# MLP of a GLA layer on one core: four rounds of 2048 hidden channels in two stages, or eight rounds of 1024 with the two projections interleaved

## The chip, the core and the metric

One NeuronCore of a Trainium2 chip. TensorE (PE) multiplies a stationary 128x128 block with moving columns and adds up in PSUM, eight banks of 128x512 float32. VectorE (DVE) and ScalarE (ACT) read PSUM and SBUF, GpSimd (POOL) does a few small things, and SyncE (SP) issues most DMAs. The metric is the device time of one execution in microseconds; lower is better.

## The reference

A gated linear attention layer and a squared-ReLU MLP over 256 tokens of width 2048, in float32. The change is in the MLP alone:

```python
def _sq_relu_mlp(h, w_up, w_down):
    a = jax.nn.relu(h @ w_up)
    return (a * a) @ w_down
...
        h = h + _sq_relu_mlp(_rmsnorm(h, mlp_norm[i]), mlp_w_up[i], mlp_w_down[i])
    return _rmsnorm(h, final_norm)
```

`w_up` is 2048 x 8192, `w_down` 8192 x 2048.

## The kernel before, in words

**Three matmuls per product.** Each float32 operand is split into a rounded part `hi` (a cast on ScalarE, L110 or L135) and a rest `lo` (a subtraction on VectorE, L111 or L136). A product is hi·hi + hi·lo + lo·hi, three matmuls of 256 columns. `halves` (L142) cuts wider products into such pieces. A weight tile (two row blocks of 512 columns, or one of 1024: 512 KB) is loaded by SP into half of one of three `raw` pairs and split into one of five slots `hi`/`lo` (`weights`, `parts`, `slots`).

**The up projection** (`turned`, L169) computes 512 hidden channels, transposed, in two banks: eight steps of two row blocks, 24 matmuls a step. `gap` stores the second half of a step's weight tile 16 elements further on; `even` lists the steps that do so. Then `up` (L622) forms the stationary blocks: for each 256 channels a ReLU and scale out of PSUM on VectorE (L628), a square on ScalarE (L632), three subtractions that make the sums (L636 to L638), and a split (L640, L641) into `act`.

**The down projection** works on units of 256 hidden channels by 512 columns, a 2x2 by 2x2 block product with 256 tokens. Plain, it takes eight block products. By sums (Strassen's method in Winograd's form) it takes seven, of sums of blocks: four sums on the stationary side (S1 to S4), four on the weight side (`u`, L680 to L685), which are split like any weights. The results lie in banks by which output block they belong to (`b32`, `b74`, `b16`, `b5`), and what can't be added at once is kept in `sums` and joined at the end (L715 to L723).

**Order.** Four rounds `r` of 2048 hidden channels. In each, `up` runs for all four groups of 512 channels; then `down` runs for the left half of the output columns and then the right one, eight hidden pairs each. In a half the first 512 columns go by sums and the second 512 plain (`blocks`, L668), 45 matmuls a pair. In round 3 the right half goes plain, as a last stage (`last_step`) that holds back its last six row blocks so that the columns come to an end one after the other, are normed and stored. Side work (transposes of h, the norm's scale, the joining) waits in a queue `side`; `pump` takes one item behind the latest split, `flush` all that are left. A framework turns the program into a fixed order per engine, by program order and its own estimate of when things are ready, and adds the semaphores.

Of the kernel before, what the change touches and what calls it, by code (L numbers as in the profile page):

```python
# [32 lines left out]
P = 128  # L33
# [28 lines left out]
ROUNDS = HID // D  # L62
# [5 lines left out]
def tile_gla_mlp(ctx, tc, x, xt, cols, w_vg, w_in, w_gate, w_out, w_up, w_down, final_norm, out):  # L68
# [7 lines left out]
    st = ctx.enter_context(tc.tile_pool(name="st", bufs=4))  # L76
# [92 lines left out]
    def turned(row, w, c0, even=(0,), acc=None):  # L169

        acc = acc or acc_banks(GT // P // 2)
        for kp in range(KT // 2):
            wh, wl = weights(w[2 * kp * P : 2 * (kp + 1) * P, c0 : c0 + GT].rearrange("(i p) c -> p i c", p=P), 2 * GT, gap=kp in even)
            for i in range(2):
                kt = 2 * kp + i
                ah, al = row(kt)
                for j in range(GT // P):
                    s = slice(j * P, (j + 1) * P)
                    o = acc[j // 2][:, j % 2 * T : (j % 2 + 1) * T]
                    for n, (u, m) in enumerate(((wh, ah), (wh, al), (wl, ah))):  # L180

                        nc.tensor.matmul(  # L182
                            o, u[:, i, s], m, start=kt == 0 and n == 0 and j % 2 == 0,
                            stop=kt == KT - 1 and n == 2, skip_group_check=True,
                        )
                if kt < KT - 1:
                    pump()
        return acc
# [44 lines left out]
    xe = mid.tile([P, 2, P], F32R, tag="xe", name="xe")  # L233
# [109 lines left out]
    gt = mid.tile([GR, T], F32R, tag="gt", name="gt")  # L343
# [240 lines left out]
    sums = [big.tile([P, 4, T], F32, tag="E" + i, name="sums", bufs=1) for i in "hl"]  # L584
    turned_h = lambda kt: [a[:, kt, :].rearrange("p (t s) -> p t s", t=NT) for a in (hth, htl)]
# [30 lines left out]
    A11, A12, A21, A22, S3, S1, S2, S4 = range(8)  # L616
    KP = KT // 2
    work = mid.tile([P, 3 * G + T], F32, tag="qt", name="work")
    r2row = work[:, 3 * G :]
    work = work[:, : 3 * G].rearrange("p (b c) -> p b c", b=3)  # L620

    def up(r, q, act):  # L622
        acc = turned(lambda kt: (hth[:, kt], htl[:, kt]), w_up, r * D + q * GT, even=() if q > 1 or r > 0 and q else (5,) if r == q == 0 else (0,))
        flush()
        f = work[:, 2].rearrange("p (f s) -> p f s", f=8)
        for b in range(2):
            s = tmp.tile([P, 2, T], F32, tag="t512", name="su", bufs=3)
            nc.vector.scalar_tensor_tensor(  # L628
                s, acc[b].rearrange("p (i t) -> p i t", i=2), 0.0, r2row.unsqueeze(1).to_broadcast([P, 2, T]),
                op0=ALU.max, op1=ALU.mult,  # L630
            )
            nc.scalar.activation(  # L632
                f[:, :4].rearrange("p (t i) s -> p i t s", t=2), s.rearrange("p i (t s) -> p i t s", t=2), AF.Square
            )
            sub = lambda o, x, y: nc.vector.tensor_tensor(o, x, y, op=ALU.subtract)
            sub(f[:, S3 : S1 + 1], f[:, A21 : A21 + 1].to_broadcast([P, 2, P]), f[:, A11 : A22 + 1 : 3])  # L636
            sub(f[:, S2], f[:, A11], f[:, S1])
            sub(f[:, S4], f[:, A12], f[:, S2])  # L638
            oh, ol = (act[q][:, b, i].rearrange("p f s -> p (f s)") for i in range(2))
            nc.scalar.copy(oh, work[:, 2])  # L640
            nc.vector.tensor_tensor(ol, work[:, 2], oh.bitcast(F32), op=ALU.subtract)  # L641

    def stationary(act, kp, f):
        return [act[kp // 2][:, kp % 2, i, f] for i in range(2)]
# [4 lines left out]
    def down(r, half, act):  # L649

        c0 = half * G
        plain = [aux_bank(), aux_bank()] if half == 0 else acc_banks(2)
        b32, b74 = acc_banks(2) if half == 0 else [aux_bank(), aux_bank()]
        b16, b5 = acc_banks(2)
        left, right = slice(0, T), slice(T, 2 * T)
        used = set()

        def product(bank, o, a, w, m, last):

            for i, (x, y) in enumerate(((0, 0), (0, 1), (1, 0))):  # L660
                halves(bank[:, o], a[x], w[y][:, m], bank.name not in used, last and i == 2)
                used.add(bank.name)

        for kp in range(KP):
            last = kp == KP - 1
            at = lambda f: stationary(act, kp, f)
            w = rows(w_down, c0, G, r * D)
            blocks = lambda i, wi: [  # L668
                product(plain[t], slice(0, 512), at((A11, A21)[t] + i), wi, slice(512, G), last and i == 1) for t in range(NT)
            ]  # L670
            assert not raw_half
            pair = wpool.tile([P, 2 * WMAX], F32, tag="raw", name="raw", bufs=3)
            raw0, raw1 = pair[:, :WMAX], pair[:, WMAX:]
            w0 = weights(w(2 * kp), G, skip=T, raw=raw0)
            product(b16, left, at(A11), w0, right, last)
            blocks(0, w0)
            pump()
            w1 = weights(w(2 * kp + 1), G, raw=raw1)
            u = work[:, kp % 2].rearrange("p (f s) -> p f s", f=4)
            add = lambda o, x, y: nc.vector.tensor_tensor(o, x, y, op=ALU.add)  # L680

            both = pair[:, T : T + 2 * (WMAX - T)].rearrange("p (k c) -> p k c", k=2)[:, :, :T]
            add(u[:, :2], raw0[:, left].unsqueeze(1).to_broadcast([P, 2, T]), both)
            add(u[:, 2], u[:, 0], raw1[:, left])
            add(u[:, 3], u[:, 2], raw1[:, right])  # L685
            wu = parts(work[:, kp % 2], G, slots())
            product(b32, right, at(A12), w1, right, last)
            product(b32, left, at(S4), w1, left, last)
            blocks(1, w1)
            product(b5, left, at(S1), wu, slice(0, T), last)  # L690
            product(b74, left, at(S3), wu, slice(T, 2 * T), last)
            product(b16, right, at(S2), wu, slice(2 * T, 3 * T), last)
            product(b74, right, at(A22), wu, slice(3 * T, G), last)
            if not last:
                pump()
        flush()
        for t in range(NT):
            take(plain[t], t, c0 + 512, 512)

        e = sums[half]  # L700
        take(b32, 0, c0, 512)
        if r == 0:
            nc.scalar.copy(e[:, 1:3].rearrange("p b c -> p (b c)"), b16)
            nc.scalar.copy(e[:, 0], b5[:, left])
            nc.scalar.copy(e[:, 3], b74[:, left])
        else:
            both = e[:, 1:3].rearrange("p b c -> p (b c)")
            nc.vector.tensor_tensor(both, b16, both, op=ALU.add)
            nc.vector.tensor_tensor(e[:, 0], b5[:, left], e[:, 0], op=ALU.add)
            nc.vector.tensor_tensor(e[:, 3], b74[:, left], e[:, 3], op=ALU.add)  # L710
        take(b74[:, right], 1, c0 + T, T)
        if r < ROUNDS - 1 - half:
            return

        tt = lambda o, x, y, op: nc.vector.tensor_tensor(e[:, o], e[:, x], e[:, y], op=op)  # L715
        tt(2, 1, 2, ALU.subtract)
        tt(0, 0, 2, ALU.subtract)
        for t in range(NT):
            if t == 1:
                tt(1, 2, 3, ALU.subtract)  # L720
# [109 lines left out]
```

## Time and profile before

| | |
|---|---|
| median of 3 runs | 1071.22 us (1070.77 to 1071.77) |
| the profiled execution | 1071.97 us, span 1070.0 us |
| TensorE busy | 1060.5 us, 9262 matmuls |
| VectorE busy | 780.3 us |
| ScalarE busy | 579.5 us |
| HBM read | 206.92 MB, 195 GB/s over the span |

TensorE's busy time is made of modelled ends of pipelined matmuls, so 99% does not yet say that matmuls follow each other closely: their starts do. The attention takes the first 382 us. The MLP's stages, in us from the start of the span: up of round 0 until about 472, then down and up alternate (down until 553, up until 640, down until 722, up until 809, down until 891, up until 978), then the last left half until about 1017 and the last stage. In rows of the timeline and the chain the first number is the start, the second the length.

### The profile page before, as it was taken

Reading aid. Unit: us, or ns where it says so; the run is one execution under the profiler, and the core shown is the slowest. Engines: PE = TensorE matmul, PEld = TensorE weight load, DVE = VectorE, ACT = ScalarE, POOL = GpSimd, SP = SyncE. Lnnn points to the kernel's source line nnn. Section 1 sums busy time; section 2 is a strip of 40 time slices with the busy share of each in tenths; the row PEclk is TensorE's granted clock in tenths of the full one; section 3 lists DMA queues with packets and bytes.
Section 4 is the critical chain, followed back from the end, with each engine's and each line's share of the span. In section 5 each row is a group of like instructions: output and inputs, shape, how many; then the busy total and the mean of one; then the engine's idle time right before and its main releaser. Section 6 shows DMA issues by size and latency. Waiting matters only on the chain.

```text
span 1070.0 us, 21834 instructions
## 1 busy us (share of the span) xinstructions
PE 1060.5 (99%) x9262; PEld 1059.9 (99%) x9262; DVE 780.3 (73%) x1039; ACT 579.5 (54%) x699; POOL 12.7 (1%) x39
## 2 busy tenths in 40 slices
PE   9999999999999999999999999999999999999997
PEld 9999999999999999999999999999999999999997
DVE  7578645556555566789976689986779997678984
ACT  7585444546444454555654556554546554555652
POOL 0000000000000000000000000000000000000000
PEclk9999999999999999999999999999999999999998
DMA  9847654556545555546565555566654566555662
GB/s 337 305 158 219 189 191 151 165 154 193 196 163 194 192 166 196 197 160 225 208 222 191 191 185 198 197 214 220 197 197 160 198 234 213 191 193 177 227 221 79
DMA packets 79569, 210.43 MB, mean 197 GB/s; under 512 B 6720, under 2 KB 7616, under 8 KB 79344
## 3 DMA queue, kind: packets, MB, share of 16 engines
q1 hardware_dynamic: 78512, 206.99, 58.5%
q10 hardware_dynamic: 960, 2.05, 0.5%
q8 instruction: 72, 1.18, 0.4%
q14 instruction: 25, 0.20, 0.1%
HBM read 206.92 MB, written 2.10 MB: 195 GB/s over the span
## 4 chain that ended last, share of the span: by engine, by line
PE 98%; issue 1%; DMA 0%; DVE 0%; ACT 0%; SPq 0%; POOLq 0%; POOL 0%; DVEq 0%; ACTq 0%
PE acc L147 44%; PE acc L182 39%; PE aux L147 12%; PE aux L182 2%; PE aux L533 1%; PE aux L462 1%; DMA raw<-in_w_vg 0%; PE acc L363 0%; DVE hf L789 0%; ACT sqf L742 0%; DVE h L647 0%; ACT hi L110 0%; POOLq L826 0%; POOL rf L297 0%; PE aux L608 0%
## 5 line engine op out<-in xcount | busy, mean ns | idle before, releaser
L111 DVE TENSOR_TENSOR lo<-raw,hi 128x1024 fp32r<-128x1024 f32 (+2 forms) x225 | 256.7, 1143 | 117.1 <-ACT hi L110 115.2
L110 ACT CAST hi<-raw 128x1024 fp32r<-128x1024 f32 (+2 forms) x225 | 222.1, 987 | 208.4 <-PE acc L147 122.4
L182 PE MATMUL acc<-hh,hi 128*128 128x256 f32 x1024 | 283.2, 277 | 0.0
L182 PE MATMUL acc<-hh,lo 128*128 128x256 f32 x1024 | 283.1, 276 | 0.0
L182 PE MATMUL acc<-hl,hi 128*128 128x256 f32 x1024 | 283.0, 276 | 0.0
L136 DVE TENSOR_TENSOR lo<-raw,hi 128x1024 fp32r<-128x1024 f32 x160 | 195.6, 1223 | 115.9 <-ACT hi L135 115.2
L135 ACT CAST hi<-raw 128x1024 fp32r<-128x1024 f32 x160 | 168.1, 1051 | 186.6 <-PE acc L182 142.2
L147 PE MATMUL acc<-hi,act 128*128 128x256 f32 x1200 | 218.1, 276 | 0.0
L182 PEld LDWEIGHTS acc<-hh,hi 128*128 128x128 f32 x1024 | 192.3, 188 | 0.0
L182 PEld LDWEIGHTS acc<-hh,lo 128*128 128x128 f32 x1024 | 192.3, 188 | 0.0
L182 PEld LDWEIGHTS acc<-hl,hi 128*128 128x128 f32 x1024 | 192.3, 188 | 0.0
L147 PEld LDWEIGHTS acc<-hi,act 128*128 128x128 f32 x1200 | 180.9, 188 | 0.0
L147 PE MATMUL acc<-lo,act 128*128 128x256 f32 x600 | 143.2, 276 | 0.0
L147 PE MATMUL aux<-hi,act 128*128 128x256 f32 x704 | 133.7, 276 | 0.0
L147 PE MATMUL acc<-hi,xA 128*128 128x256 f32 x736 | 106.9, 282 | 0.6 <-ACT hi L110 0.6
L147 PEld LDWEIGHTS aux<-hi,act 128*128 128x128 f32 x704 | 106.6, 188 | 0.0
L147 PEld LDWEIGHTS acc<-lo,act 128*128 128x128 f32 x600 | 102.4, 188 | 0.0
L147 PEld LDWEIGHTS acc<-hi,xA 128*128 128x128 f32 x736 | 95.2, 190 | 1.1 <-ACT hi L110 0.9
L110 ACT CAST hi<-work 128x1024 fp32r<-128x1024 f32 x56 | 59.1, 1056 | 37.5 <-PE aux L147 13.9
L147 PE MATMUL aux<-lo,act 128*128 128x256 f32 x352 | 76.3, 276 | 0.0
L111 DVE TENSOR_TENSOR lo<-work,hi 128x1024 fp32r<-128x1024 f32 x56 | 68.3, 1220 | 9.4 <-ACT hi L110 7.5
L147 PE MATMUL acc<-lo,xA 128*128 128x256 f32 x368 | 60.1, 281 | 0.0
(162 smaller groups left out, 1275.9 us busy)
## 6 DMA issues: line engine op xcount, KB each, us to landing
raw<-in_w_up SPq DMA_DIRECT2D x128, 512.0 KB, 4.5
raw<-in_w_down SPq DMA_DIRECT2D x128, 512.0 KB, 4.4
raw<-in_w_in SPq DMA_DIRECT2D x80, 512.0 KB, 4.6
raw<-in_w_out SPq DMA_DIRECT2D x32, 512.0 KB, 4.1
raw<-in_w_vg SPq DMA_DIRECT2D x13, 520.0 KB, 8.7
h<-in_x SPq DMA_DIRECT2D x4, 512.0 KB, 7.2
zz<-in_xt SPq DMA_DIRECT2D x3, 384.0 KB, 7.9
fb<-in_final_norm ACTq DMA_DIRECT2D x1, 1024.0 KB, 7.0
```

Of the source, the lines that this page charges most:

```text
L110: last_hi[0] = nc.scalar.copy(hi[:, s], raw[:, s])
L111: last_lo[0] = nc.vector.tensor_tensor(lo[:, s], raw[:, s], hi[:, s].bitcast(F32), op=ALU.subtract)
L135: last_hi[0] = nc.scalar.copy(to[0], dst)
L136: last_lo[0] = nc.vector.tensor_tensor(to[1], dst, to[0].bitcast(F32), op=ALU.subtract)
L147: nc.tensor.matmul(o[:, m], x, w[:, m], start=first and c == 0, stop=last, skip_group_check=True)
L182: nc.tensor.matmul(o, u[:, i, s], m, start=kt == 0 and n == 0 and j % 2 == 0, stop=kt == KT - 1 and n == 2, skip_group_check=True,)
L462: nc.tensor.matmul(o, kab[:, k[0], c0 + c, k[1] : k[1] + P], q(qt[:, c0 + c]), start=c == 0, stop=c == 1)
L533: nc.tensor.transpose(b[:, i * T + t * P : i * T + (t + 1) * P], src[:, t, kt * P : (kt + 1) * P], ident)
```

## The change

A round now has 1024 hidden channels, two groups of 512 of the up projection and four hidden pairs; there are eight rounds. `turned` becomes a generator that yields after each of its eight steps (`turned_steps`), and `up` runs through all rounds with it. `down` is a generator too: it walks through passes (round, column group of 512), in alternating direction, and yields after each unit of four per pass. A loop first takes 18 up steps and then one up step behind every unit, until the up steps are used up. The up groups after the first collect in the two `aux` banks instead of two of the six `acc` banks; a pass uses four `acc` banks, which stay in use where a round starts with the column group that the last one ended with. Which units go by sums is given by `by_sums`: the first three of four hidden pairs, two in column group 1, and three of the eight units in round 7. Each column group has its own `sums` tile; its four banks are emptied with four operations of 512 columns. Columns 1024 and up of round 7 are the last stage, eight row blocks, six of them held. The blocks of `act` are in another order so that pairs which go plain need only half of it. `xe` and `gt` share one tile, and the ring `st` has three buffers instead of four.

```diff
+MR = 2 * GT
+ROUNDS = HID // MR
...
-    st = ctx.enter_context(tc.tile_pool(name="st", bufs=4))
+    st = ctx.enter_context(tc.tile_pool(name="st", bufs=3))
...
+    def turned_steps(row, w, c0, even, acc, flip=0):
         for kp in range(KT // 2):
             wh, wl = weights(w[2 * kp * P : 2 * (kp + 1) * P, c0 : c0 + GT].rearrange("(i p) c -> p i c", p=P), 2 * GT, gap=kp in even)
...
+                    k = j % 2 ^ flip
+                    o = acc[j // 2][:, k * T : (k + 1) * T]
...
                 if kt < KT - 1:
                     pump()
+            yield
...
+    sums += [mid.tile([P, 4, T], F32, tag=i, name="sums") for i in ("db", "ee")]
...
+    def order_of(m):
+
+        return range(GROUPS)[:: 1 if m % 2 else -1]
+
+    def by_sums(m, g, kp):
+
+        if m == ROUNDS - 1:
+            return (g, kp) in ((0, 0), (0, 2), (1, 0))
+        return kp < (2 if g == 1 else 3)
+
+    def up():
+        for m in range(ROUNDS):
+            for q in range(MR // GT):
+                first = m == q == 0
+                acc = acc_banks(2) if first else [aux_bank(), aux_bank()]
+                even = (5,) if first else (0,) if m == 0 else (3,) if q == 0 else ()
+                yield from turned_steps(lambda kt: (hth[:, kt], htl[:, kt]), w_up, m * MR + q * GT, even, acc, 1)
+                if m == 0:
+                    flush()
...
+                for b in range(2):
+                    forms(m, 2 * q + b, acc[b], act[:, b])
+
+    def forms(m, kp, bank, act):
+        ways = {by_sums(m, g, kp) for g in range(GROUPS)}
...
+        if True in ways:
...
+            sub(f[:, S3 : S1 + 1], f[:, A21:].to_broadcast([P, 2, P]), f[:, A11 : A22 + 1])
+            sub(f[:, S2], f[:, A11], f[:, S1])
+            sub(f[:, S4], f[:, A12], f[:, S2])
...
+        some = slice(0 if True in ways else A12, 8 if False in ways else A21)
...
+    def down(passes):
+
+        for n, (m, g) in enumerate(passes):
+            if not n or passes[n - 1][1] != g:
+                b32, bx4, b16, b57 = acc_banks(4)
+            ends = n + 1 == len(passes) or passes[n + 1][1] != g
+            for kp in range(KP):
...
+                src = w_down[c0 : c0 + 2 * P, g * GT : (g + 1) * GT].rearrange("(i p) c -> p i c", p=P)
+                last_load[0] = nc.sync.dma_start(out=raw.rearrange("p (i c) -> p i c", i=2), in_=src)
+                if not by_sums(m, g, kp):
+                    w = parts(raw, 2 * GT, slots())
+                    for i in range(2):
+                        for bank, f in ((b32, (A11, A12)), (bx4, (A21, A22))):
+                            product(bank, slice(0, GT), at(f[i]), w, slice(i * GT, (i + 1) * GT))
+                    yield
+                    continue
+                w = parts(raw, 2 * GT, slots(), [(T, 2 * GT)])
...
+                add(u[:, :2], raw[:, :1].to_broadcast([P, 2, T]), raw[:, 1:3])
+                add(u[:, 2], u[:, 0], raw[:, 2])
+                add(u[:, 3], u[:, 2], raw[:, 3])
+                wu = parts(wk, G, slots())
...
+                product(b16, left, at(A11), w, block(1))
+                product(b32, right, at(A12), w, block(3))
+                product(b32, left, at(S4), w, block(2))
+                product(b57, left, at(S1), wu, block(0))
+                product(b57, right, at(S3), wu, block(1))
+                product(b16, right, at(S2), wu, block(2))
+                product(bx4, right, at(A22), wu, block(3))
+                yield
+            if ends:
+                take(b32, 0, g * GT, GT)
+                take(bx4, 1, g * GT, GT)
...
+                for dst, bank in ((e[:, 1:3], b16), (e[:, 0::3], b57)):
...
+                        nc.vector.tensor_tensor(dst, b, dst, op=ALU.add)
...
+                if m == ROUNDS - 1 or m == ROUNDS - 2 and g > 1:
+                    side.extend(combine(g))
...
+    passes = [(m, g) for m in range(ROUNDS) for g in order_of(m) if m < ROUNDS - 1 or g < 2]
+    steps = up()
+    for _ in range(KT + 2):
+        next(steps)
+    for _ in down(passes):
+        next(steps, None)
...
+    acc = [[aux_bank(), aux_bank()], acc_banks(3)]
+    KL = MR // P
     LAST, ROOM = 6, 2
...
+    for kt in range(KL):
+        k = kt - KL + ROOM
...
+        if kt < KL - LAST:
...
+        pump(3)
```

175 lines of the change are left out of this document (65 added, 110 removed).

## The prediction

> **What bounds the kernel now.** The page comes first, for the engine that is full. Its line 1 gives the time, the number of matmuls and the load of VectorE (DVE); its part 4 says which engine the end hangs on.
>
> ```profile
> span 1070.0 us, 21834 instructions
> PE 1060.5 (99%) x9262; PEld 1059.9 (99%) x9262; DVE 780.3 (73%) x1039; ACT 579.5 (54%) x699; POOL 12.7 (1%) x39
> ...
> PE 98%; issue 1%; DMA 0%; DVE 0%; ACT 0%; SPq 0%; POOLq 0%; POOL 0%; DVEq 0%; ACTq 0%
> ```
>
> TensorE carries 98% of the chain, but its busy ends are modelled, so the question is whether its matmuls follow each other as closely as they can. For that I read the chain in order of time, whose columns are start, length and the matmuls merged in the piece.
>
> ```profile
> 386.40 5.07 PE acc L182 x43
> ...
> 397.98 73.77 PE acc L182 x649
> ...
> 517.64 1.70 PE acc L147 x15
> ...
> 522.75 1.70 PE acc L147 x15
> ...
> 553.35 87.12 PE acc L182 x768
> ...
> 722.07 87.12 PE acc L182 x768
> ...
> 1017.34 36.73 PE acc L147 x324
> 1056.49 7.03 issue
> ```
>
> From 553.35 to 722.07 is one whole round, up and down: 168.72 us. It holds 768 up matmuls and 720 down ones (16 hidden pairs of 45), so one takes 168.72/1488 = 0.1134 us. The pure up piece (87.12/768 = 0.1134) and the last down piece (36.73/324 = 0.1134) agree. So in the MLP from 398 us on, TensorE never waits; time can come only from fewer matmuls, or be lost by new waits. The rest stays: 382 us of attention in front, and some 8 us behind the last matmul.
>
> A second rate is in the first rows: at 386.40, 43 matmuls take 5.07 us, 0.1179 each. This slow spacing begins among the transposes of h and is over in the piece from 397.98. What ends it is the step whose weight tile has a gap between its halves (the list `even`): such a step has twelve matmuls 0.12 apart, as here in the round that starts at 553.35, and the fast spacing holds after it.
>
> ```profile
> 554.54 0.28 PE L182 MATMUL acc<-hh,hi 128*128 128x256 f32 x1
> 554.66 0.28 PE L182 MATMUL acc<-hl,hi 128*128 128x256 f32 x1
> 554.78 0.28 PE L182 MATMUL acc<-hh,lo 128*128 128x256 f32 x1
> ```
>
> The next engine is VectorE. Windows over one up and one down stage:
>
> ```profile
> 553.35:640.47 87.12, 87.12 (x770) 87.12 (x770) 60.81 (x75) 42.93 (x47) 0.00 (x0) 1.00 0.61 201
> 640.47:722.07 81.60, 81.60 (x722) 81.60 (x722) 77.38 (x106) 50.29 (x52) 0.00 (x0) 1.00 0.59 199
> ```
>
> The columns are window, length, then busy time and count of PE, PEld, DVE, ACT, POOL, then the granted clock, DMA share and GB/s. In the down stage VectorE is busy 77.38 of 81.60 us (95%) and TensorE still loses nothing; in the up stage it is at 70%. ScalarE is at 62% at most and the DMA engines at 61%.
>
> **Fewer matmuls.** A unit is 256 hidden rows by 512 output columns; the down projection has 32 x 4 = 128 of them. Plain, a unit takes 24 matmuls (8 block products of 3); by sums, 21. Before, 7 half passes of 8 units go by sums: 56. After, rounds 0 to 6 have 3+2+3+3 = 11 each, round 7 has 3: 80. So 24 more units save 3 matmuls each: 72 x 0.1134 = 8.16 us. The up projection keeps its 3072. The Trainium skill (TensorE: Matmul & The Clock Gate, "Wait — 56ns, not 53.3ns?") gives N/2.4 GHz plus about 2.5 ns per warm matmul; by that estimate, 109.2 ns for 256 columns, the saving would be 7.86 us, but the rows here show 113.4 ns and the measurement decides.
>
> **Gapped steps.** Before, `even` names two in round 0 and one in each of three rounds: 5. After: two in round 0, one in each of seven: 9. Each costs 12 x (0.12 - 0.1134) = 0.08 us, so +0.32 us. They are paid by TensorE itself, so nothing hides them.
>
> **VectorE's load.** The durations, by line and shape:
>
> ```profile
> L111 DVE TENSOR_TENSOR lo<-raw,hi 128x1024 fp32r<-128x1024 f32 x150 | 183.3, 1223 | 102.6 <-ACT hi L110 102.0
> ...
> L111 DVE TENSOR_TENSOR lo<-raw,hi 128x768 fp32r<-128x768 f32 x56 | 53.4, 953 | 4.4 <-ACT hi L110 3.4
> ...
> L680 DVE TENSOR_TENSOR work<-work,raw 128x256 f32<-128x256 f32 x112 | 46.7, 417 | 0.2
> ...
> L680 DVE TENSOR_TENSOR work<-raw 128x512 f32<-128x512 f32 x56 | 38.3, 684 | 2.0 <-DMA raw<-in_w_down 1.8
> ...
> L628 DVE SCALAR_TENSOR_TENSOR su<-acc,work 128x512 f32<-128x512 f32 x32 | 21.1, 688 | 0.0
> ...
> L635 DVE TENSOR_TENSOR work<-work 128x128 f32<-128x128 f32 x64 | 18.6, 290 | 1.6
> ```
>
> Neighbours overlap, so what counts is start to start, in VectorE's timeline:
>
> ```profile
> 510.37 0.68 DVE L647 TENSOR_TENSOR h<-acc,h 128x512 f32<-128x512 f32 x1
> 510.97 1.22 DVE L111 TENSOR_TENSOR lo<-work,hi 128x1024 fp32r<-128x1024 f32 x1
> 512.10 1.28 DVE L647 TENSOR_TENSOR h<-aux,h 128x512 f32<-128x512 f32 x2
> ```
> ```profile
> 515.43 1.22 DVE L111 TENSOR_TENSOR lo<-raw,hi 128x1024 fp32r<-128x1024 f32 x1
> 516.57 1.22 DVE L111 TENSOR_TENSOR lo<-work,hi 128x1024 fp32r<-128x1024 f32 x1
> 517.70 0.42 DVE L680 TENSOR_TENSOR work<-work,raw 128x256 f32<-128x256 f32 x1
> 518.04 0.95 DVE L111 TENSOR_TENSOR lo<-raw,hi 128x768 fp32r<-128x768 f32 x1
> 518.91 0.68 DVE L680 TENSOR_TENSOR work<-raw 128x512 f32<-128x512 f32 x1
> ```
>
> 1024 columns 1.14 us, 768 columns 0.87, 512 columns 0.60, 256 columns 0.34; 128 columns then about 0.21 (290 ns less the same 0.08 of overlap). One hidden pair of before costs 0.87 + 1.14 + 0.60 + 0.34 + 0.34 + 1.14 = 4.43 us beside 45 matmuls, 5.10 us. The new pairing, one up step (24 matmuls, 1.14 us of VectorE) with one unit by sums (21 matmuls; 0.87 + 0.60 + 0.34 + 0.34 + 1.14 = 3.29), is the same 45 matmuls and the same 4.43 us. An up step with a plain unit is 48 matmuls, 5.44 us, beside 2.28 us.
>
> Two costs come on top. Forming the stationary blocks: 0.60 + 0.34 + 0.42 + about 1.0 to 1.14 = 2.3 to 2.5 us per hidden pair, 1.2 where all its units are plain: about 8.4 us in a round of four pairs. Emptying the banks: four operations of 512 columns, 2.4 us, at each change of column group; a round starts with the group that the last one ended with, so there are three per round and 23 in all. Per round VectorE does 11 x 4.43 + 5 x 2.28 + 8.4 + 7.2 = 75.7 us, and TensorE (384 + 11 x 21 + 5 x 24) x 0.1134 = 83.3 us. That is 91%, less than the down stage already runs at. Over the whole kernel VectorE's busy time should rise by some 70 us, to about 850: 24 x 2.15 more for the sums, about 30 more for emptying and joining, 13 less for forming. I price it at nothing on average.
>
> **Where it comes in bursts.** How far VectorE is ahead can be read: the 768-column part that ends at 518.99 is used by the x15 piece at 522.75, a lead of 3.8 us. After a group's last up step it must empty both aux banks (0.60 each) before the next up step; the down unit between, 2.38 us or more, covers that. If a bank is late, the up step waits, and the next down unit behind it on TensorE's queue too. But the whole forming (4.7 us for the first up group's two pairs) and, one unit later, the 2.4 us of emptying fall close together. From the end of the up group TensorE has a unit by sums, an up step, a plain unit, an up step and 9 matmuls, 2.38 + 2.72 + 2.72 + 2.72 + 1.02 = 11.56 us, until it needs the summed weights of the next column group's first unit. Until then VectorE owes 4.7 + 2.4 and the splits 1.14 + 0.87 + 1.28 + 1.14 = 4.4: 11.5 us. So it fits with nothing to spare in the rounds whose second column group has three units by sums (0, 2, 4, 6); in the others the units there are plain and leave a microsecond or more. Lower end: 0, and not below, since TensorE has no wait in the MLP that could go. Upper end: the lead is gone before it starts, 4.7 - 3.8 = 0.9 us and more a round, about 7 us. I take 1.5 us, four rounds at 0.4, near the lower end because the existing down stage empties its banks at 95% load without a loss.
>
> **Edits with one answer.** The w_down loads become 512 columns of two row blocks, the shape of w_up:
>
> ```profile
> raw<-in_w_up SPq DMA_DIRECT2D x128, 512.0 KB, 4.5
> raw<-in_w_down SPq DMA_DIRECT2D x128, 512.0 KB, 4.4
> ```
>
> They land in the same time, the count stays 128, and SP issues them in the same order as they are used: 1 MB per 5.10 us, as now. ScalarE gets 24 more 1024-column casts and loses some forming; at 62% that is hidden. Eighteen up steps run ahead; between the second group of round 0 and the first of round 1 no down unit covers the hand-over of the aux banks, 0.60 us once at most. In the last ten units no up step runs, and a unit by sums asks 3.29 us of VectorE for 2.38 of TensorE; round 7 therefore has only three, between plain units (1.14 for 2.72), and nothing is lost. The last stage keeps its six held rows; VectorE must join both column groups and scale them (8 x 0.34 + 8 x 0.60 = 7.5 us) beside eight splits (9.1 us) in 21.8 us. The joined gate tile and the smaller `st` ring touch only the attention, where their neighbours are several microseconds apart: 0.
>
> **Sum**, against the profiled execution (1071.97 us, 0.75 above the median of the runs, 1071.22): -8.16 + 0.32 + 1.5 = -6.3, which is 1065.6 there and 1064.9 on the median; I say 1065.0.
>
> **Rivals.** A change under 0.2%, 2.1 us, can't be told from none here. The first rival leans on one more row of VectorE's timeline, from the change of halves:
>
> ```profile
> 513.90 0.95 DVE L111 TENSOR_TENSOR lo<-raw,hi 128x768 fp32r<-128x768 f32 x1
> ```
>
> *VectorE's bursts stall TensorE* (the one that ends slower). For it: the sum above leaves 0.1 us, each queue keeps a fixed order, and the forming, which nobody needs for many units, may stand ahead of a split that is due at once. Against it: 95% without a loss. The lead at the change of halves was only 2.8 us (the 768-column part started at 513.90 and is used at 517.64). If every forming burst starts from 2.8 us, 8 x (4.7 - 2.8) + 8 x (3.7 - 2.8) = 22 us, and the result is 1085. It decides from about 0.5 us per burst, where 16 of them eat the 7.8 us.
>
> *The slow spacing takes hold.* If the many changes between up steps and down units, or a wait, put the matmuls in the 0.1179 state, with a gapped step to end it once a round only: half a round's up matmuls, and more, at 4.5 ns. For the 2688 up matmuls of rounds 1 to 7 that is 12 us, and the time 1075.5. Against it: the changes at 475, 553 and 722 us left the spacing at 0.1134.
>
> *The clock falls at the hand-over of the two aux banks.* The first matmuls of the execution run at half pace, two from 6.71 to 7.14:
>
> ```profile
> 6.71 0.63 PE L147 MATMUL acc<-lo,xA 128*128 128x256 f32 x2
> 7.14 1.49 PE L147 MATMUL acc<-hi,xA 128*128 128x256 f32 x6
> ```
>
> If each of 15 hand-overs costs one up step at that pace, 15 x 24 x 0.1 = 36 us, and the time about 1100. The Trainium skill (TensorE: Matmul & The Clock Gate, "A second HAM failure mode: psum-queue depth-cycling") tells of cycling banks with small idle times that makes the clock swing. The trace speaks against it as far as it goes: in the MLP, bank changes cost nothing.
>
> *The saving is real but is given back at the ends*, at the start of the down units and in the shorter last stage: 1070, no change to be told.
>
> **Chances.** Forecast (cover holds, 1063 to 1069): 0.68. Bursts: 0.18, of which 0.05 end within 0.2% and 0.13 slower. Slow spacing: 0.06, slower. Clock: 0.03, slower. Given back at the ends: 0.05, same. So faster 0.68, same 0.10, slower 0.22. The range goes from 1062.8 (no stall at all is 1063.4, less 0.6 for the spread of the runs) to 1077, which takes in the slow spacing and the milder bursts; what is left out is the worse bursts and the clock, about 0.13. The forecast's own range is 1062.8 to 1069.
>
> **What would show it.** Right: 9190 matmuls; 80 instead of 56 splits of sums; about 0.1134 us per matmul over a whole round of 83.3 us; DVE near 850 us; no matmul group with idle time before it. Wrong: rows of PE waiting for DVE `lo` or for an aux bank's reader each round; 0.1179 spacing over long stretches; chain pieces of DVE in the MLP; a gap before the last stage.

## The result and the profile after

The changed kernel takes 1081.37 us (median of four, 1079.66 to 1085.54); the kernel before took 1071.49 us beside it. The ratio is 1.0101, with a 95% interval of 1.0086 to 1.0115. So the change makes the kernel slower by about 10 us, where the prediction had it faster by 6.

Page of the changed kernel, its line 1 and its part 4:

```profile
span 1079.3 us, 21887 instructions
PE 1065.0 (99%) x9190; PEld 1063.1 (99%) x9190; DVE 837.5 (78%) x1161; ACT 592.6 (55%) x725; POOL 12.7 (1%) x39
...
PE 85%; DVE 6%; DMA 5%; issue 2%; ACT 1%; SPq 0%; DVEq 0%; POOLq 0%; POOL 0%; ACTq 0%
```

The 72 matmuls are gone (9190), and the "busy" 99% of TensorE shows nothing. The chain does: VectorE (DVE) and DMA now hold 11% of it, before they held nothing. That is not lost time as such: from each of two waits of TensorE the chain runs back through VectorE and the loads for some 60 us, while TensorE still has work. Windows of 84 us, about a round each; the columns are window, length, then busy time and count of PE, PEld, DVE, ACT, POOL, the granted clock, DMA share and GB/s:

```profile
530.00:614.00 84.00, 84.00 (x743) 84.00 (x742) 75.71 (x104) 48.61 (x52) 0.00 (x0) 1.00 0.65 203
614.00:698.00 84.00, 83.92 (x719) 83.72 (x718) 75.75 (x106) 46.44 (x51) 0.00 (x0) 1.00 0.65 199
698.00:782.00 84.00, 84.00 (x716) 84.00 (x715) 74.65 (x102) 46.37 (x50) 0.00 (x0) 1.00 0.65 200
950.00:1034.00 84.00, 79.92 (x657) 79.18 (x657) 77.10 (x112) 41.87 (x47) 0.00 (x0) 0.96 0.60 186
```

Look at the count of PE, not at its busy time: 743 matmuls in an undisturbed round, 716 to 719 in two rounds that look just as full, and 657 in the last, where the granted clock is 0.96. There are thus two kinds of loss, waits and a slower pace without any wait.

**The waits.** The chain around one of them (start, length, what), and VectorE's timeline for the same stretch (in brackets the idle time before the instruction and what ended it):

```profile
625.27 1.15 DVE lo L137
626.42 0.02 issue
626.43 4.16 DMA raw<-in_w_down
...
632.85 1.15 DVE lo L112
634.00 0.04 issue
634.04 0.97 PE acc L148 x6
635.02 2.83 PE aux L183 x24
```
```profile
630.69 0.69 DVE L723 TENSOR_TENSOR work<-raw 128x512 f32<-128x512 f32 x1 [2.28 <-DMA raw<-in_w_down]
631.30 1.22 DVE L137 TENSOR_TENSOR lo<-raw,hi 128x1024 fp32r<-128x1024 f32 x1
632.44 0.42 DVE L723 TENSOR_TENSOR work<-work,raw 128x256 f32<-128x256 f32 x1
632.77 1.22 DVE L112 TENSOR_TENSOR lo<-raw,hi 128x1024 fp32r<-128x1024 f32 x1
633.91 0.68 DVE L661 SCALAR_TENSOR_TENSOR su<-aux,work 128x512 f32<-128x512 f32 x1
```

The split of an up step (L137) frees a pair of raw buffers; the w_down load that was waiting for it goes out at 626.43 and lands 4.16 us later. VectorE's next instruction, the first weight sum of a later unit, needs that load, and stands still for 2.28 us. Behind it in the fixed order stands the split of the plain unit that TensorE is about to use (632.77, L112): TensorE waits for it, 0.25 us. In round 0 the same instructions stand in the same order, but the load is there in time, and TensorE does not wait:

```profile
461.46 0.69 DVE L723 TENSOR_TENSOR work<-raw 128x512 f32<-128x512 f32 x1
...
463.54 1.22 DVE L112 TENSOR_TENSOR lo<-raw,hi 128x1024 fp32r<-128x1024 f32 x1
```

Nor is it the last load alone. The chain has no piece of TensorE between 573.94 and 634.04, so VectorE and the loads set the pace all that time. In these 60 us VectorE is busy for 52.27 and stands for 6.4 before six w_down loads; nothing is left of its lead at the end:

```profile
574.00:634.00 60.00, 59.96 (x529) 59.76 (x527) 52.27 (x72) 33.89 (x36) 0.00 (x0) 1.00 0.62 193
DVE work L723 <- DMA raw<-in_w_down: 6.4, 6, 2.3
```

At 973 us the same order costs 2 us; here two operations of the joining (L755) stand ahead of the split as well:

```profile
971.10 0.69 DVE L723 TENSOR_TENSOR work<-raw 128x512 f32<-128x512 f32 x1 [1.55 <-DMA raw<-in_w_down]
...
972.84 0.75 DVE L755 TENSOR_TENSOR sums<-sums 128x256 f32<-128x256 f32 x2
...
973.85 1.22 DVE L112 TENSOR_TENSOR lo<-raw,hi 128x1024 fp32r<-128x1024 f32 x1
```
```profile
972.60 0.73 PE L148 MATMUL acc<-hi,act 128*128 128x256 f32 x5
975.12 0.50 PE L148 MATMUL acc<-lo,act 128*128 128x256 f32 x2 [1.79 <-DVE lo L112]
...
977.18 0.41 PE L183 MATMUL aux<-hl,hi 128*128 128x256 f32 x1
...
979.31 0.40 PE L183 MATMUL aux<-hh,lo 128*128 128x256 f32 x1
```

The third place is the end of the MLP, where up steps have run out: TensorE waits for a cast of ScalarE, which stands behind another cast that had waited 6.01 us for VectorE's weight sums. No load is in play here: VectorE is busy without a gap from 1016.97 to 1027.81 us, with the forming of the last up group among the sums.

```profile
1027.05 1.05 ACT L111 CAST hi<-work 128x1024 fp32r<-128x1024 f32 x1 [6.01 <-DVE work L723]
```
```profile
1029.83 0.50 PE L148 MATMUL acc<-hi,act 128*128 128x256 f32 x2 [1.84 <-ACT hi L111]
1030.78 0.58 PE L148 MATMUL acc<-hi,act 128*128 128x256 f32 x1 [0.44 <-ACT act L676]
```

**What follows a wait.** Soon after the waits at 973 and 1027 us come 15 and 14 matmuls 0.213 us apart (rows 977.18 to 979.31 above), half the pace, for about 3 us; that is the granted clock of 0.96 in the last window. The Trainium skill (TensorE: Matmul & The Clock Gate, "What's actually happening") gives half rate after an idle window of about 3.4 us. The half pace agrees, but here waits of some 2 us were followed by it already.

And then the spacing stays slow. The chain's pieces of one up step, 24 matmuls each:

```profile
571.21 2.73 PE aux L183 x24
...
635.02 2.83 PE aux L183 x24
...
693.55 2.86 PE aux L183 x24
...
780.15 2.84 PE aux L183 x24
...
785.37 2.72 PE aux L183 x24
```

Before the short wait at 633.7 a step takes 2.72 to 2.73 us, after it 2.83: 0.1178 us a matmul in place of 0.1133. The gapped step at 693.55 does not end this, the one at 780.15 does. After 979 us it holds until about 1020 us, and from 1031 us to the last matmul.

**The account**, from the starts of all matmuls after 380 us, one profiled execution against the other (spans 1079.3 and 1070.0). A wait is the distance of two starts less the usual 0.11:

| | us |
|---|---|
| 72 matmuls fewer | -8.16 |
| four more gapped steps | +0.32 |
| waits at 633.7 and 973 (0.25 + 1.96) | +2.2 |
| waits from 1027 to 1031 | +3.0 |
| 29 matmuls at half pace | +2.9 |
| slow spacing, in three stretches (634 to 782, 979 to 1020, 1031 to 1071), less that of before | +8.4 |
| smaller gaps | +0.6 |
| sum | +9.3 |

### The profile page after: what moved, and what is told of

Read it like the earlier page. It is cut to its first block, busy times and chain, and to the rows that moved or that the text cites. A ratio compares the mean times of both kernels' runs of the same rounds, so it can differ in the third digit from the quotient of the medians.

```text
span 1079.3 us, 21887 instructions
## 1 busy us (share of the span) xinstructions
PE 1065.0 (99%) x9190; PEld 1063.1 (99%) x9190; DVE 837.5 (78%) x1161; ACT 592.6 (55%) x725; POOL 12.7 (1%) x39
## 4 chain that ended last, share of the span: by engine, by line
PE 85%; DVE 6%; DMA 5%; issue 2%; ACT 1%; SPq 0%; DVEq 0%; POOLq 0%; POOL 0%; ACTq 0%
PE acc L148 46%; PE aux L183 27%; PE acc L183 8%; DMA raw<-in_w_down 4%; PE aux L148 2%; DVE lo L137 2%; DVE lo L112 1%; DVE work L723 1%; DMA zz<-in_xt 1%; PE aux L541 1%; PE aux L470 1%; DVE h L683 1%; DMA raw<-in_w_vg 0%; ACT hi L111 0%; DVE sums L747 0%
## 5 line engine op out<-in xcount | busy, mean ns | idle before, releaser
L112 DVE TENSOR_TENSOR lo<-raw,hi 128x768 fp32r<-128x768 f32 (+3 forms) x225 | 249.5, 1113 | 101.1 <-ACT hi L111 100.7
L148 PE MATMUL acc<-hi,act 128*128 128x256 f32 x1808 | 319.3, 278 | 2.3 <-ACT hi L111 1.8
L111 ACT CAST hi<-raw 128x768 fp32r<-128x768 f32 (+3 forms) x225 | 216.2, 963 | 165.0 <-PE acc L148 128.5
L148 PEld LDWEIGHTS acc<-hi,act 128*128 128x128 f32 x1808 | 270.5, 188 | 2.7 <-ACT hi L111 2.0
L183 PE MATMUL aux<-hl,hi 128*128 128x256 f32 x960 | 266.1, 278 | 0.0
L183 PE MATMUL aux<-hh,hi 128*128 128x256 f32 x960 | 266.0, 278 | 0.0
L183 PE MATMUL aux<-hh,lo 128*128 128x256 f32 x960 | 264.4, 278 | 0.0
L137 DVE TENSOR_TENSOR lo<-raw,hi 128x1024 fp32r<-128x1024 f32 x160 | 194.9, 1219 | 38.0 <-ACT hi L136 37.7
L183 PEld LDWEIGHTS aux<-hl,hi 128*128 128x128 f32 x960 | 181.0, 188 | 0.0
L183 PEld LDWEIGHTS aux<-hh,hi 128*128 128x128 f32 x960 | 180.9, 189 | 0.0
L183 PEld LDWEIGHTS aux<-hh,lo 128*128 128x128 f32 x960 | 179.8, 188 | 0.0
L112 DVE TENSOR_TENSOR lo<-work,hi 128x1024 fp32r<-128x1024 f32 x80 | 97.6, 1219 | 21.6 <-ACT hi L111 10.8
L723 DVE TENSOR_TENSOR work<-raw 128x512 f32<-128x512 f32 x80 | 55.0, 688 | 35.5 <-DMA raw<-in_w_down 35.3
```

What stands on the lines that cost most here:

```text
L111: last_hi[0] = nc.scalar.copy(hi[:, s], raw[:, s])
L112: last_lo[0] = nc.vector.tensor_tensor(lo[:, s], raw[:, s], hi[:, s].bitcast(F32), op=ALU.subtract)
L137: last_lo[0] = nc.vector.tensor_tensor(to[1], dst, to[0].bitcast(F32), op=ALU.subtract)
L148: nc.tensor.matmul(o[:, m], x, w[:, m], start=first and c == 0, stop=last, skip_group_check=True)
L183: nc.tensor.matmul(o, u[:, i, s], m, start=kt == 0 and n == 0 and j % 2 == 0, stop=kt == KT - 1 and n == 2, skip_group_check=True,)
```

## The experiments

Three theories at first. A: VectorE comes late because it stands still behind w_down loads that go out late, since two loads share a pair of raw buffers. B: VectorE has simply too much to do where forming and emptying meet. C: most of what is lost is the aftermath of waits, whatever causes them. The expectations call C theory S; their A2 is A with VectorE's order, and not the late load alone, as the cause. Ratios are against the kernel before on the same chip, whose median lay between 1070.60 and 1070.81 us.

### Fewer units by sums: 8, 9 and 10 of 16

```diff
-        return kp < (2 if g == 1 else 3)
+        return kp < 2                              # 8 of 16
+        return kp < (3 if g == 3 else 2)           # 9 of 16
+        return kp < (2 if g in (1, 2) else 3)      # 10 of 16
```

> The changed kernel with the first two of four hidden pairs by sums in every column group of rounds 0 to 6: 8 of 16 units instead of 11, 59 in all. 63 more matmuls, 7.1 us. If the load of the sums on VectorE makes the waits (A and B alike): no TensorE wait, no slow spacing after the transposes of h, 1070 to 1071 us. If the interleaving itself makes them, whatever the load: the waits stay and the time is 1085 to 1090 us.

> The changed kernel with 9 of 16 units by sums (three hidden pairs in column group 3 alone): 42 more matmuls than the change, 4.8 us, without any wait 1068.2 us. Expected of both theories: no TensorE wait, 1068 to 1069 us, a little faster than before.

> The changed kernel with 10 of 16 units by sums (two hidden pairs in column groups 1 and 2, three in 0 and 3): 21 more matmuls than the change, 2.4 us, without any wait 1065.8 us. VectorE 73.5 us a round instead of 75.7. Theory B and A alike have fewer waits; if VectorE's slack decides gradually, half of the 18 us of waits and slow spacing stay, about 1074 us; if it is a threshold that lies between 10 and 11, 1066 to 1067 us.

| units by sums in rounds 0 to 6 | matmuls saved | without any stall | measured | lost |
|---|---|---|---|---|
| 8 | 9 | 1070.1 | 1070.32 (1070.00 to 1071.53) | 0.2 |
| 9 | 30 | 1067.6 | 1071.16 (1067.52 to 1073.48) | 3.6 |
| 10 | 51 | 1065.2 | 1072.01 (1067.55 to 1076.09) | 6.8 |
| 11 (the change) | 72 | 1063.7 | 1081.37 (1079.66 to 1085.54) | 17.7 |

"Without any stall" is the median of before on the same chip, less 0.1134 us for each matmul saved, plus 0.32. Interleaving as such costs nothing that shows: with 8 units the ratio is 0.9993 (0.9984 to 1.0003), though VectorE waits for w_down loads there too, 23.7 us in all. The ninth and the tenth unit bring nothing (ratios 1.0002, 0.9989 to 1.0015, and 1.0011, 0.9994 to 1.0028), and the eleventh costs 9 us more. In the traced run with nine units no two starts in the MLP are more than 0.23 us apart; most of what it loses is slow spacing, from 804 to 865 us. The windows show what changes: VectorE's 69.31 us of 84 with eight units against 75.75 with eleven.

```profile
614.00:698.00 84.00, 84.00 (x743) 84.00 (x742) 69.31 (x90) 44.95 (x48) 0.00 (x0) 1.00 0.66 200
```

### Single raw buffers

```diff
-        a = wpool.tile([P, 2 * WMAX], F32, tag="raw", name="raw", bufs=3)
-        return a[:, :WMAX], a[:, WMAX:]
+        return [wpool.tile([P, WMAX], F32, tag="raw", name="raw", bufs=6)]
```

> The changed kernel with six single raw buffers in place of three pairs (same memory), so that a half is loaded again as soon as its own split has read it and not when its neighbour's has. Theory A (VectorE stands in its fixed order before an addition whose w_down load has not landed, because the pair came free late): VectorE's waits on w_down loads fall from 35.3 us to under 10, the TensorE waits at 634, 973 and 1028 us go, and with them the slow spacing; 1063 to 1067 us. Theory B (of the prediction: the bursts of forming and emptying are more than VectorE's lead): loads that come earlier change nothing; TensorE waits as before, 1078 to 1084 us.

1082.01 us (1079.88 to 1085.51), ratio 1.0103 (1.0079 to 1.0128): no gain. The w_down loads now land 7.5 us ahead of their cast (median from 440 to 950 us; 4.4 with the change), yet VectorE still waits for them, and TensorE, in other rounds, for `su`:

```profile
DVE work L722 <- DMA raw<-in_w_down: 47.5, 43, 3.4
...
PE aux L182 <- DVE su L660: 4.8, 3, 1.9
```
```profile
721.58 0.69 DVE L722 TENSOR_TENSOR work<-raw 128x512 f32<-128x512 f32 x1 [1.50 <-DMA raw<-in_w_down]
...
723.32 1.28 DVE L660 SCALAR_TENSOR_TENSOR su<-aux,work 128x512 f32<-128x512 f32 x2
```

(The first fence is from the list of waits: who waits for whom, us in total, times, longest; the second is VectorE's timeline.) Where the load is earlier the weight sum is ordered earlier too, and again something that TensorE needs at once, here `su`, which empties an aux bank, stands behind it. Theory A in its plain form falls.

### Weight sums held back behind the up step's split

```diff
+                behind = last_lo[0].ins
-                add(u[:, :2], raw[:, :1].to_broadcast([P, 2, T]), raw[:, 1:3])
+                with tc.issue_after(behind):
+                    add(u[:, :2], raw[:, :1].to_broadcast([P, 2, T]), raw[:, 1:3])
```

The other two sums stand in the same block.

> The changed kernel with one change of VectorE's order: the additions that make a unit's weight sums stand behind the split of the up step before them, not ahead of it. Theory A2 (VectorE has time enough, 75.7 of 84 us, but spends 35 us in front of additions whose load has just been issued, with a split that TensorE needs standing behind them): its waits on w_down loads fall under 10 us, the TensorE waits shrink from 8.7 us to under 2, 1064 to 1069 us. Theory B (bursts beyond the lead): the waits on loads go but TensorE waits at the same places, 1078 to 1084 us.

> The same order together with six single raw buffers. Theory A2: as the run before or up to 1 us better, 1063.5 to 1068 us, since a late load can no longer hold VectorE. Theory B: 1078 to 1084 us.

1100.76 us (1098.25 to 1101.32) with pairs and 1099.42 (1098.11 to 1099.98) with single buffers, ratios 1.0277 and 1.0271. VectorE no longer waits for loads, but now sum, cast and split of one unit follow each other on two engines with nothing between, and both wait:

```profile
ACT hi L111 <- DVE work L724: 228.9, 71, 6.4
DVE lo L112 <- ACT hi L111: 159.8, 148, 1.9
```

So the early place of the sums has its use: it gives the cast its time. To hold all of them back is no remedy, and the wait for a load is not by itself what costs.

### More gapped steps

```diff
-                even = (5,) if first else (0,) if m == 0 else (3,) if q == 0 else ()
+                even = (5,) if first else (0,) if m == 0 else (1, 5)
```

> The changed kernel with two gapped up steps in every group of rounds 1 to 7 instead of one per round: 30 in place of 9. Theory S (most of the loss is the spacing of 0.118 us that follows a wait and lasts until a gapped step): the waits stay, the time at slow spacing falls from about 200 us to under 80, 8.7 us of loss to about 3, less 1.7 us for the 21 gapped steps: 1076 to 1078 us. If the slow spacing is not ended by gapped steps, or is not the loss: 1081 to 1084 us.

1081.75 us (1081.36 to 1082.07), ratio 1.0098 (1.0083 to 1.0113). Over the MLP, what lies above 0.1134 us a matmul is 6.8 us of slow spacing and gapped steps where the change has 8.7, but 12.3 us of waits and half pace where it has 9.2. With less of the aftermath TensorE comes sooner to where VectorE is late: seven waits in place of five. So this run can't tell what the aftermath alone is worth.

### One wait put into the kernel before

```diff
+                n_step[0] += 1
+                if n_step[0] == DELAY_AT:
+                    for _ in range(9):
+                        nc.vector.tensor_tensor(to[1], dst, to[0].bitcast(F32), op=ALU.subtract)
```

It repeats a split of one up step of round 1 nine times, so that TensorE waits once.

> The kernel before, with nine extra copies of one VectorE split in up group 1 of round 1 (fourth step): some 10 us of VectorE, about 1 to 4 us more than its lead, so that TensorE waits there once. Theory S: from that wait on matmuls are 0.118 us apart until the gapped step at the start of round 2, about 120 us later: 4.5 to 5 us beside the wait itself, 1077 to 1081 us. If a wait costs only itself: 1072 to 1075 us and a spacing of 0.1134 right behind it.

1087.9 us in one run (span 1086.0). TensorE's timeline at the wait, and the chain later on:

```profile
591.84 0.58 PE L188 MATMUL acc<-hh,lo 128*128 128x256 f32 x1 [9.52 <-DVE lo L142]
592.22 0.41 PE L188 MATMUL acc<-hh,hi 128*128 128x256 f32 x1
```
```profile
727.34 1.77 PE acc L153 x15
...
737.94 22.11 PE acc L188 x194
```

The wait is 9.7 us; then some 20 matmuls go at 0.213 us, and from there to about 740 us each takes 0.118 (1.77/15) until a gapped step of the next round ends it (22.11/194 = 0.114). That stretch costs 5.4 us; with the wait and the half pace (20 x 0.1 us) it makes up the 17 us. The wait is 9.7 us and not the 1 to 4 that were expected, which puts the time above both ranges. Theory C is right as to its kind: in a kernel that has nothing of the change, one wait was followed by 5.4 us of slow spacing.

### Forming spread out, and one more step ahead

The square, the sums and the split of a forming go into the queue of side work, one piece behind each later split (first edit); 19 up steps run ahead in place of 18 (second edit).

```diff
+            side.extend([nothing, sums_of, nothing, nothing, split])
...
-    for _ in range(KT + 2):
+    for _ in range(KT + 3):
```

> The changed kernel with the forming spread out: the ReLU that frees the aux bank stays where it is, the square with its subtractions and the split of the blocks become side work, one piece every few pumps over the next up steps. The same instructions, the same total. Theory B: no burst of 4.7 us, so no TensorE wait and no slow spacing after it: 1063 to 1068 us. Theory A: 1078 to 1083 us.

> The changed kernel with 19 up steps ahead instead of 18, nothing else: the forming then falls one unit earlier, away from the emptying at the end of a column group. Theory B (TensorE waits where the forming of an up group and the emptying of a column group meet on VectorE): the waits go or halve, 1065 to 1074 us. Theory A (VectorE loses its slack evenly, by its fixed order and its waits on loads): no change, 1079 to 1083 us.

> The forming spread out and 19 up steps ahead. Theory B: as the run before, 1063 to 1067 us. Theory A: 1078 to 1083 us.

> The forming spread out, with 10 of 16 units by sums: without any wait 1065.8 us. Theory B: 1066 to 1067 us, with a narrower spread than the 1067.6 to 1076.1 of 10 of 16 alone. Theory A: as that, about 1072 us.

| | median (range) | ratio (95%) |
|---|---|---|
| forming spread, 18 ahead | 1077.88 (1074.01 to 1081.75) | 1.0068 (1.0041 to 1.0096) |
| forming as in the change, 19 ahead | 1066.44 (1065.11 to 1071.58) | 0.9969 (0.9956 to 0.9982) |
| forming spread, 19 ahead | 1065.94 (1064.44 to 1071.64) | 0.9959 (0.9946 to 0.9972) |
| forming spread, 18 ahead, 10 of 16 units | 1070.63 (1068.44 to 1075.33) | 1.0007 (0.9994 to 1.0020) |

With one step more ahead the same instructions give back almost all; spreading the forming at 18 steps leaves most of the loss. The third row has the lowest median here, but the intervals of the second and third overlap. In the third, TensorE keeps the pace of a stall-free round, with VectorE as busy as ever; the chain on its page, and its window:

```profile
PE 96%; DMA 1%; issue 1%; ACT 0%; SPq 0%; DVE 0%; POOLq 0%; POOL 0%; DVEq 0%; ACTq 0%
```
```profile
614.00:698.00 84.00, 84.00 (x743) 84.00 (x742) 77.57 (x107) 47.62 (x53) 0.00 (x0) 1.00 0.63 203
```

Theory B falls as it stands: here VectorE is busy for 77.57 us of 84, and TensorE does not wait. How much VectorE has to do does not decide alone, though it counts in the order of the change, as 8 to 11 units showed; what stands where counts as well.

### Is it the place of the forming, or the lead? 17 and 20 steps ahead

```diff
-    for _ in range(KT + 2):
+    for _ in range(KT + 1):      # 17
+    for _ in range(KT + 4):      # 20
```

> Seventeen up steps ahead: the forming of a round's first group stands directly ahead of the emptying, with no unit between. Both theories expect more waits than with 18: 1081 to 1095 us. A time of 1075 us or less would speak against both.

> Twenty up steps run ahead instead of 18. The forming of a round's first group then stands one unit behind the emptying of a column group (with 19 ahead: two units before the next one; with 18: one unit before it). If its place decides, emptying and forming crowd again and the gain is lost again, wholly or in part: 1071 to 1082 us, with waits of TensorE on VectorE's lo or su in several rounds. If the lead decides, one more step ahead is at least as good as 19: 1063.5 to 1067 us and almost no waits.

17 ahead: 1068.06 us (1064.32 to 1072.44), ratio 0.9972 (0.9955 to 0.9989). 20 ahead: 1076.56 (1074.74 to 1082.44), ratio 1.0065 (1.0043 to 1.0088). That is against both: with the smallest lead, and the forming directly at the emptying, the kernel is fast. The largest wait with 20 has the same form in a new place. The chain, at the change from the first round's up steps to the second's:

```profile
422.67 4.11 DMA raw<-in_w_down
...
426.81 0.70 DVE work L723
...
429.43 0.61 DVE su L661
```

A load goes out late, a weight sum waits for it, and behind the sum stands the `su` that would free the aux bank: TensorE waits 3.6 us and runs at half pace for 26 matmuls after.

### Is it how the loads are paired?

An odd number of steps ahead also shifts the pairs: w_up then w_down share one, where the change has w_down then w_up. One edit shifts the pairs alone, at 18 and at 19 steps; another takes single buffers at 19.

```diff
+    raw_half.extend(raw_pair()[1:])
     steps = up()
```

> Eighteen steps ahead as in the change, but one half of a raw pair is left out ahead of the up steps, so that each pair holds a w_up load and then a w_down load, as with 17 and 19. If the pairing decides: 1065 to 1069 us, w_down landing about 7 us before its cast (4.4 with the change). If the number of steps ahead decides (where the forming falls): 1078 to 1084 us.

> Nineteen steps ahead, with pairs that hold a w_down load and then a w_up load, as in the change. If the pairing decides: 1075 to 1084 us. If the number of steps ahead decides: 1065 to 1068 us.

> Nineteen steps ahead with six single raw buffers. With 18 ahead, single buffers gave 1082.0 us. If the pairing w_up then w_down is what helps, single buffers lose it: 1075 to 1083 us. If the number of steps ahead decides: 1065 to 1068 us.

Medians of all arrangements with the forming as in the change:

| steps ahead | w_down opens the pair | w_up opens the pair | single buffers |
|---|---|---|---|
| 17 | not tried | 1068.06 | not tried |
| 18 | 1081.37 (the change) | 1067.97 | 1082.01 |
| 19 | 1067.93 | 1066.44 | 1069.09 |
| 20 | 1076.56 | not tried | not tried |

The ranges at 18 shifted, 19 shifted and 19 single are 1066.53 to 1072.85, 1066.17 to 1071.77 and 1065.34 to 1072.34; the ratios 0.9984 (0.9967 to 1.0001), 0.9977 (0.9965 to 0.9989) and 0.9983 (0.9967 to 0.9999). One unused half buffer is worth 13 us at 18 steps. But neither pairing nor lead decides alone: each of them was enough where the other was bad. Nor is it decided by how early the loads land. With the pairs shifted at 18 steps the w_down loads land 7.5 us ahead of their cast, as with the slow single buffers; at 19 steps with w_down first they land 4.5 us ahead, as in the slow change. VectorE's timeline with 18 steps and shifted pairs, at the same place of the same round as 630 us above:

```profile
626.75 0.69 DVE L723 TENSOR_TENSOR work<-raw 128x512 f32<-128x512 f32 x1 [0.83 <-DMA raw<-in_w_down]
...
630.55 1.22 DVE L112 TENSOR_TENSOR lo<-raw,hi 128x1024 fp32r<-128x1024 f32 x1
631.69 0.68 DVE L723 TENSOR_TENSOR work<-raw 128x512 f32<-128x512 f32 x1
632.29 1.28 DVE L661 SCALAR_TENSOR_TENSOR su<-aux,work 128x512 f32<-128x512 f32 x2
```

VectorE waits for a load here as well (0.83 us), but a unit earlier, and the plain unit's split (630.55) now stands ahead of the next weight sum (631.69), which waits for no load. In the change that sum came first. The framework fixes this order from its own estimate of when things are ready, and the edits that were compared give it other orders.

### Gapped steps in the fastest version

> Spread forming and 19 steps ahead (single times before: 1064.4 to 1071.6 us), now with two gapped steps in each up group of rounds 1 to 7, 28 in place of 7, which cost 21 x 0.08 = 1.7 us of TensorE. If the upper times come from slow spacing that goes on until a gapped step, the times draw together at about 1065 to 1067.5 us. If they come from waits, the spread stays and the median rises by the 1.7 us to 1067.5 or more.

The edit is the same line `even` as above, in the version with spread forming and 19 steps. 1067.26 us (1065.80 to 1067.95), ratio 0.9967 (0.9956 to 0.9979). The times draw together, from a range of 7.2 us to one of 2.2, and the median rises by 1.3 where the added gapped steps alone cost 1.7. This is what stretches of slow spacing of varying length would give. Of this version no execution at the upper end was traced, but of the one with single buffers and 19 steps one was, at 1071.93 us in a range of 1065.34 to 1072.34. No two starts in its MLP are more than 0.25 us apart, and from 798 to 947 us it runs at the slow spacing, 716 matmuls in 84 us:

```profile
800.00:884.00 84.00, 84.00 (x716) 84.00 (x715) 74.71 (x102) 47.30 (x51) 0.00 (x0) 1.00 0.64 195
```

## Why the prediction was wrong

From profile to profile -6.3 us was forecast, and +9.3 came. The saving was right. The step that failed is the price of VectorE's bursts: 1.5 us in the middle and "nothing is lost" at the end, with a wait that costs only its own length. In its place the runs showed 5.2 us of waits, and behind them 2.9 us at half pace and 8.4 us of slow spacing, for which the sum had no term.

- **Fewer matmuls, -8.16 us, and gapped steps, +0.32**: right. 9190 matmuls, 0.1133 us each where nothing waits. The fastest version lies 3.1 us above the time without any stall (1070.60 - 8.16 + 0.32 = 1062.8).
- **VectorE's load, 75.7 us a round**: right to 1.1 us (75.71, 75.75 and 74.65 in the windows); in total 837.5 where it had 850. The price of "nothing on average" holds for the load by itself: the version with spread forming and 19 steps runs at 77.57 of 84 us without a wait. It does not hold in the order of the change, where VectorE and its loads set the pace for 60 us ahead of a wait, and where the loss falls from 17.7 us to 0.2 as three units a round go back to plain.
- **Where it comes in bursts, +1.5 us**: the place was right: the forming of the first group in rounds 2 and 6, of the four rounds it named. The waits there were 2.2 us, near the 1.5. But it counted only what VectorE owes, and not what stands still: the order may put an instruction that waits for a DMA ahead of one that TensorE needs. VectorE waited 35.3 us for w_down in the change, and 1.8 before:

```profile
DVE work L723 <- DMA raw<-in_w_down: 35.3, 42, 2.3
```

  With 2.28 us of such a wait in the stretch, 11.5 us owed in 11.56 can't hold. The sum of these waits does not decide by itself: with 19 steps and w_down first it is 36.9 us, in a kernel whose median is 1067.93 us.
- **Edits with one answer, the w_down loads**: "land in the same time" was right for w_down (4.3 us; w_up took 5.2 where it had 4.5), but the row that mattered is when they go out, not how long they take. That two loads of different haste now share a pair, and that the pair comes free with its later reader, was not looked at. Which of them opens the pair was worth 13 us at 18 steps; but buffers that share nothing gave none of it back (1082.01), so the shared pair alone does not explain it.
- **Round 7, "nothing is lost"**: wrong by 3.0 us of waits and 1.4 at half pace. The step set three units by sums against their plain neighbours and left out the forming of the last up group, which VectorE does between them; and it weighed VectorE alone, while ScalarE's queue stood for 6.01 us before the cast of one weight sum with the casts of plain units behind it. Also not in the sum: the joining of column groups 2 and 3 falls in round 6, 5.1 us by the prediction's own prices (2 x (4 x 0.34 + 2 x 0.60)), beside the wait at 973 us.
- **The rivals**: the first named the kind of mechanism ("may stand ahead of a split that is due at once") and its sign, with 0.18; but it had the forming standing there, where the trace shows a weight sum that waits for its load, and its 22 us were 5.2 us of waits. The second, slow spacing, had 0.06, and it took 8.4 us, the largest term of the loss; it was set beside the first as if each came alone, when the one can set off the other. The third, the clock, came too, but after waits and not at hand-overs: 2.9 us. A wait should have been priced with its aftermath, which the rows at 386.40 and 6.71 us in the prediction already showed as states.

## What to carry to other kernels

When one engine paces a kernel and another feeds it at 90%, read the feeder's order and not only its load: look for an instruction that waits for a just-issued DMA ahead of one that the pacing engine needs next, and change what makes the order (which transfers share a buffer, how many steps run ahead) before cutting work. Price a wait of TensorE with what follows it; here the aftermath cost more than the waits. And where times hang on such an order, try its neighbours: from 17 to 20 steps ahead, the same instructions gave 1066 to 1082 us.

## What the runs showed of the hardware

- TensorE has two steady spacings for these 256-column matmuls, 0.1133 and 0.1178 us. A wait of 0.25 us was followed by the slow one for 148 us, 9.7 us of wait in the kernel before for about 145 us. A gapped step can end it (780.15) and can fail to (693.55). What tells the two apart is open; in the run with 18 steps and shifted pairs a slow stretch began at 802 us with no wait above 0.05 us.
- Half pace (0.213 us) set in after ten waits, between starts 1.79 us apart and more, and lasted 14 to 26 matmuls; after starts 1.76 us apart or less it did not, and once not after 2.03 us.
- What stays open of the cause: which pair of VectorE's instructions would have to change places to keep 18 steps and the pairs of the change. That was read from the traces; an order with that alone exchanged was not tried.
